# Spreading the turn of the latents and the first residual scaling in a transformer block on one Trainium2 core

## The chip, the core and the metric

The kernel runs on one core of a Trainium2 chip. A core has four engines that compute, each with its own instruction queue that is worked off in order: TensorE (matmuls and transposes, into PSUM; PE in the profile), VectorE (DVE), ScalarE (ACT) and GpSimd (POOL). SyncE (SP) issues loads from memory into the on-chip SBUF; POOL and ACT issue some as well. The engines wait for one another by semaphores. The metric is the time of one execution in microseconds (us) on the device. The unchanged kernel took 2508.15 us (median of 3 runs, 2506.3 to 2508.43).

## What is computed

One layer of a streaming encoder over 256 tokens of width 2048, in float32:

```python
h = layer_norm(ALPHA * h + 0.5 * swiglu_ffn(h, ffn1...), ln_ffn1_g, ln_ffn1_b)
mix = hybrid_mixer(h, ...)
h = layer_norm(ALPHA * h + mix, ln_mix_g, ln_mix_b)
xa = memory_cross_attention(h, mem, ...)
h = layer_norm(ALPHA * h + xa, ln_x_g, ln_x_b)
h = layer_norm(ALPHA * h + 0.5 * swiglu_ffn(h, ffn2...), ln_ffn2_g, ln_ffn2_b)
```

The mixer has two attention branches. Branch A has 16 heads of width 64 over q, k and v projected directly from h, with a relative-position bias. Branch B (latent attention) first projects h to two latents of width 512, one for q and one for k and v, and normalises each:

```python
c_q = rms_norm(q_lat, q_a_norm)     # y = x * rsqrt(mean(x^2) + eps) * gain
c_kv = rms_norm(kv_lat, kv_a_norm)
```

Its 16 heads are projected from c_q and c_kv. The outputs of both branches are gated, added and projected.

## The kernel before

Each float32 weight is split into a high part in TensorE's reduced format and the low remainder: ScalarE casts the high part (`hi`, L242, two casts of 128x1024) and VectorE subtracts it from the loaded tile to get `lo` (L245, one instruction of 128x2048). A product is then a run of `hi` matmuls and a run of `lo` matmuls. There are three load buffers (`raw`) and two each of `hi` and `lo`, so a cast has to wait until TensorE has finished the `hi` matmuls of two units earlier.

The program is a list of items, each a Python function with the weights that it needs. `add` appends one, and `run` goes through the list in order and emits the loads and splits a little ahead of the item that uses them. `add` takes `prio`: instructions emitted with SOON (400) or NEAR (100) are preferred by the framework's scheduler, which fixes each engine's order when the kernel is built, and those with LATE (-400) go behind. `held` counts weight units that an item keeps, which limits how far `run` loads ahead.

Around the change the items are, in this order:
- the projection to both latents (`w_lat`), and `lat_scale` (L849-865), which leaves the two latents, divided by their root mean square, as `self.lat`, token-major;
- `gb_apply(0, self.h)` (L434-445), with prio LATE. The residual `h` (two tiles of 128 tokens by 2048) holds the first LayerNorm's result without scale and offset, and here it gets them in place. For each quarter of 512 columns POOL loads the scale and the offset, spread over the partitions, into two work tiles (L440, L441; 256 KB each), and VectorE multiplies (L444) and adds (L445) for both token tiles. `h` is next used after the mixer's output projection;
- `kpe`: the rotary key shared by the B heads (L892-899). `swap` (L890) exchanges its halves by four small DMAs on SP's queue, and L898 waits for them;
- `a_proj(0)`, the q and k projections of the first pair of A heads (16 `hi` matmuls at L265, 16 `lo` matmuls at L267 for each), and then `lat_turn` (L868-881);
- a loop over the eight pairs of A heads: projections of the next pair, transpose of the probabilities of the pair before (L773, copied out by ScalarE at L779), scores (L921) with a softmax, output (L962, L963);
- the 16 B heads in the same manner: `b_scores` (L921, then L1037 and a softmax on VectorE and ScalarE that ends with L768), `b_trans` (L773), `b_proj` (L255, L286), `b_out` (L962, L963).

`lat_turn` transposes the latents to feature-major and applies the RMS gains: for each of the two latents and each half of its 512 features one PSUM tile is filled by two pairs of 128x128 transposes (L876). Behind each pair ScalarE multiplies by the gain into the high part (L880) and VectorE forms the low part (L881). The second pair of a tile writes the same PSUM tile as the first, and it waits until the L881 of the first pair has read it. The result `self.c` lies in the blocks X0 and X1 and is first needed by the B heads' projections. PSUM has four tiles of this kind (`at`), shared with scores, probabilities and outputs.

The work tiles `w2` (128x512) are a ring of five: the softmax tile of each head, the transposed probabilities, and both loads of a quarter in `gb_apply` come from it.

Of the kernel before, what the change touches and what calls it, by code (L numbers as in the profile page):

```python
# [17 lines left out]
P = 128  # L18
S = 256
# [27 lines left out]
SOON, NEAR, LATE = 400, 100, -400  # L47
# [44 lines left out]
class Kernel:  # L92
# [338 lines left out]
            return [scale], [quarters((0, 1))], [quarters((2, 3))]  # L431
        return steps

    def gb_apply(self, i, h):  # L434

        nc = self.nc
        for q in range(4):
            cs = slice(q * 512, (q + 1) * 512)
            g, b = self.w2(), self.w2()
            nc.gpsimd.dma_start(g, self.t["gb"][i, 0:1, cs].to_broadcast([P, 512]))  # L440
            nc.gpsimd.dma_start(b, self.t["gb"][i, 1:2, cs].to_broadcast([P, 512]))  # L441
            for tt in range(2):
                hs = h[tt][:, cs]
                nc.vector.tensor_tensor(hs, hs, g, ALU.mult)  # L444
                nc.vector.tensor_tensor(hs, hs, b, ALU.add)  # L445
# [337 lines left out]
    def mixer(self, xT, st, steps):  # L783
        nc, t = self.nc, self.t
# [24 lines left out]
        ps = {}  # L809
# [3 lines left out]
        a, b, c = steps(1)  # L813
# [51 lines left out]
                    else:  # L865
                        nc.scalar.mul(l, l, r)

        def lat_turn():  # L868
            self.c = self.act(["X0", "X1"])
            for k in range(2):  # L870
                for b in range(2):
                    ps = self.at_tile()
                    for i in range(2):
                        j, p = 2 * b + i, ps[:, i * S:(i + 1) * S]
                        for tt in range(2):
                            nc.tensor.transpose(p[:, tt * P:(tt + 1) * P],  # L876
                                                self.lat[:, tt, k, j * P:(j + 1) * P], self.ident)
                        gain = self.vec(("q_a_norm", "kv_a_norm")[k], j)
                        hi, lo = (self.c.at(half, 4 * k + j) for half in (0, 1))
                        nc.scalar.mul(hi, p, gain)  # L880
                        nc.vector.scalar_tensor_tensor(lo, p, gain, hi.bitcast(F32), ALU.mult, ALU.subtract)  # L881

        self.pair_group(0, t["w_lat"][0], 512, KT, xT, SUMS_IN, fx, lps, lqs, None, SUM_HOME + ("H5",))
        self.add(lat_scale, prio=SOON)
        self.add(lambda: self.gb_apply(0, self.h), prio=LATE)

        def swap(dst, src):

# [14 lines left out]
        qk, sc, pt = {}, {}, {}  # L903
        oA = {}

        def a_proj(i):
            def one(k):
                def fn(w):
                    ps = self.mm_tile()
                    self.mm_wide(ps, w, xT())  # L910
                    qk[i, k] = self.total(ps)
                return fn
            for k in range(2):
                self.add(one(k), t["w_qk"][i, k])

        def scores(parts, spans_q):

            ps = self.at_tile()
            for c0, tt, nk in spans_q:
                for j, (q, k) in enumerate(parts):  # L920
                    nc.tensor.matmul(ps[:, c0:c0 + nk], q[:, tt * P:(tt + 1) * P], k[:, :nk],  # L921
                                     start=(j == 0), stop=(j == len(parts) - 1))
            return ps
# [15 lines left out]
        def a_scores(i):  # L939
            def fn():  # L940
                load_rel(i + 1)
                for j in range(2):
                    bias = rel["t"][:, i % 2, j, :]
                    rows = slice(64 * j, 64 * j + 64)
                    ps = scores([(qk[i, 0][rows], qk[i, 1][rows])], CAUSAL)
                    s = self.w2()
                    with self.prio(NEAR):
                        nc.vector.scalar_tensor_tensor(s[:, :3 * P], ps[:, :3 * P], 1.0 / math.sqrt(A_DIM), bias,
                                                       ALU.mult, ALU.add)
                        self.softmax(s, SPANS)  # L950
                    sc[i, j] = s
            self.add(fn)

        def a_trans(i):
            def fn():
                for j in range(2):
                    pt[i, j] = self.transpose_p(sc.pop((i, j)), (0, P, 2 * P))
            self.add(fn)

        def pv(ps, v, pT):  # L960

            nc.tensor.matmul(ps[:, :S], v(0), pT[:, :S], start=True, stop=False)  # L962
            nc.tensor.matmul(ps[:, P:S], v(1), pT[:, S:S + P], start=False, stop=True)  # L963

        def a_out(i):
            def fn():
                if i == 0:
                    oA["t"] = self.act(["H5", "X2"])
                ps = self.at_tile()
                for j in range(2):  # L970
                    c = (2 * i + j) * A_DIM
                    pv(ps[64 * j:64 * j + 64], lambda kt: va["t"][:, kt, c:c + A_DIM], pt.pop((i, j)))
                self.split(ps[:, :S], oA["t"].at(0, i), oA["t"].at(1, i))
            self.add(fn)
# [3 lines left out]
        for g in range(2):  # L978
            def fn(w, g=g):
                if g == 0:  # L980
                    self.rt = self.block("T0")
                for j in range(4):
                    ps = self.mm_tile()
                    self.mm_feat(ps[:, :S], w, [j * 512 + k * P for k in range(4)], self.c, range(4))
                    (nc.scalar.copy if j % 2 else nc.vector.tensor_copy)(self.rt[:, 4 * g + j, :], ps[:, :S])
# [11 lines left out]

        self.add(lambda: load_rel(0))
        a_proj(0)
        self.add(lat_turn)  # L1000
        NA = A_HEADS // 2
        bq, bsc, bpt, bv, oB, kept = {}, {}, {}, {}, {}, {}

        def b_proj(h):
            def vfn(w, g=h // 4):
                if g == 0:
                    bv["t"] = self.block("X3", (P, 2, 2, 512))
                for tt in range(2):
                    ps = self.mm_tile()
                    self.mm_tok(ps, tt, w, self.c, range(4, 8), True, True)  # L1010
                    (nc.scalar.copy if tt else nc.vector.tensor_copy)(bv["t"][:, g % 2, tt, :], ps)
            if h % 4 == 0:
                self.add(vfn, t["w_v"][h // 4])

            def fn(w=None):

                if h % 2 == 0:
                    kept[h + 1] = w
                else:
                    w = kept.pop(h)  # L1020
                for k in range(2):
                    ps = self.mm_tile()
                    c = h % 2 * 1024 + k * 512
                    self.mm_feat(ps[:, :S], w, [c + j * P for j in range(4)], self.c, range(4 * k, 4 * k + 4))
                    v = self.w1()
                    (nc.scalar.copy if k == 0 else nc.vector.tensor_copy)(v, ps[:, :S])
                    bq[h, k] = v
            self.add(fn, *(() if h % 2 else (t["w_nope"][h // 2],)), held=h % 2)
# [14 lines left out]
        def b_trans(h, held):  # L1043
            def fn():
                bpt[h] = self.transpose_p(bsc.pop(h), (0, P, 2 * P))
            self.add(fn, held=held)

        def b_out(h, held):
            def fn():
                if h == 0:  # L1050
                    oB["t"] = self.act(["T1", "T2", "T3", "H4"])
                ps = self.at_tile()
                pv(ps, lambda kt: bv["t"][:, h // 4 % 2, kt, h % 4 * P:h % 4 * P + P], bpt.pop(h))
                self.split(ps[:, :S], oB["t"].at(0, h), oB["t"].at(1, h))
            self.add(fn, held=held)


        for i in range(NA + 1):
            if i + 1 < NA:
                a_proj(i + 1)  # L1060
            if i > 0:
                a_trans(i - 1)
            if i < NA:
                a_scores(i)
            if i == NA - 2:
                self.items += rope_items
            if i == NA - 1:
                b_proj(0)
                b_proj(1)
            if i > 0:  # L1070
                a_out(i - 1)
        for h in range(B_HEADS + 1):

            held = int(h % 2 and h + 2 < B_HEADS)
            if h < B_HEADS:
                b_scores(h, held)
            if h > 0:
                b_trans(h - 1, held)
            if h + 2 < B_HEADS:
                b_proj(h + 2)  # L1080
            if h > 0:
                b_out(h - 1, int(h % 2 == 0 and h + 2 < B_HEADS))


        mix, fb = Act([]), {}
# [50 lines left out]
        side = self.mem_norm()  # L1136
# [322 lines left out]
```

## Time and profile before

The profile is of one execution. It lists the busy time of each engine, then waits, a timeline per engine and the share of the chain that ended last.

| what | value |
|---|---|
| runs | 2506.3, 2508.43, 2508.15 us |
| profiled execution, span from first to last instruction | 2508.1 us |
| TensorE busy | 2484.0 us (99%) |
| VectorE busy | 2055.5 us (82%) |
| ScalarE busy | 1334.4 us (53%) |
| mean granted TensorE clock | 0.997 |

In the timeline a row is: start, length, engine, line, operation, output<-input, partitions x elements, count, and in brackets how long the engine was idle before and what released it. Consecutive instructions of one kind are merged into a row, and records of neighbouring rows overlap a little, as instructions are pipelined. In the windows view a row is a stretch, its length, and for TensorE, its weight loads, VectorE, ScalarE and GpSimd the busy time with the number of instructions; then the granted TensorE clock (1.00 is full speed), the busy share of the DMA queues, and GB/s. A wait row says who waited for whom: us in total, number of times, the longest. A DMA row ends with KB of each transfer and us from issue to landing. Line numbers are those of the kernel before; in the changed kernel lines from L869 on move by one, those behind `a_proj` by three.

### The profile page before, as it was taken

The page shows a single profiled execution, that of the slowest core. Times are in us where ns is not written, and L with a number is a line of the kernel's source. Part 1 is how long each engine was busy: PE and PEld are TensorE (multiplying, and loading weights), DVE is VectorE, ACT ScalarE, POOL GpSimd, SP SyncE. Part 2 cuts the span into 40 slices and gives each one's busy share as a digit, 9 for nine tenths or more (in the row PEclk, how much of TensorE's full clock was granted, in tenths as well). Part 3 has the DMA queues.
Part 4 walks back from the last instruction along what each step waited for, and adds up shares of the span by engine and source line. Part 5 has one row for each costly group of instructions (what it writes and reads, how often), then busy time and mean ns, then how long its engine had stood idle before and what let it go on. Part 6 is the DMA issues. An engine that isn't in the chain of part 4 may idle for free.

```text
span 2508.1 us, 30455 instructions
## 1 busy us (share of the span) xinstructions
PE 2484.0 (99%) x11966; PEld 2082.5 (83%) x11966; DVE 2055.5 (82%) x2312; ACT 1334.4 (53%) x1798; POOL 28.3 (1%) x67
## 2 busy tenths in 40 slices
PE   9999999999999999999999999999999999999998
PEld 8888888889888887888888888888888888888886
DVE  6999889899778988676578798557888988898986
ACT  5555555555455555554444564545555555555552
POOL 0000000000000001000000000000000000000000
PEclk9999999999999999999999999999999999999999
DMA  6655555546645556543456547544554555555553
GB/s 254 240 197 204 189 202 203 207 174 220 233 159 202 208 204 223 182 150 113 154 208 231 187 171 253 195 155 149 211 205 171 203 199 201 201 201 201 200 214 141
DMA packets 72512, 490.03 MB, mean 195 GB/s; under 512 B 8368, under 2 KB 8752, under 8 KB 17200
## 3 DMA queue, kind: packets, MB, share of 16 engines
q1 hardware_dynamic: 66384, 467.11, 51.7%
q0 software_dynamic: 4256, 17.83, 2.2%
q10 hardware_dynamic: 1728, 3.15, 0.3%
q8 instruction: 93, 1.52, 0.2%
q14 instruction: 51, 0.42, 0.0%
HBM read 484.77 MB, written 2.10 MB: 194 GB/s over the span
## 4 chain that ended last, share of the span: by engine, by line
PE 94%; DVE 3%; DMA 2%; ACT 0%; issue 0%; SPq 0%; DVEq 0%; POOL 0%; ACTq 0%; POOLq 0%
PE mm L299 25%; PE at L299 24%; PE mm L353 10%; PE at L353 9%; PE mm L286 8%; PE mm L265 7%; PE mm L267 4%; PE mm L255 2%; PE at L921 2%; DVE lo L245 1%; PE at L286 1%; PE at L773 1%; DMA H<-xT 0%; PE at L1275 0%; PE at L962 0%; PE at L404 0%
## 5 line engine op out<-in xcount | busy, mean ns | idle before, releaser
L242 ACT CAST hi<-raw 128x1024 fp32r<-128x1024 f32 (+1 forms) x848 | 801.9, 988 | 603.7 <-PE at L299 178.5
L245 DVE TENSOR_TENSOR lo<-raw,hi 128x2048 fp32r<-128x2048 f32 (+2 forms) x425 | 904.5, 2129 | 239.2 <-ACT hi L242 237.4
L299 PE MATMUL mm<-hi,T 128*128 128x512 f32 (+1 forms) x1280 | 298.5, 383 | 0.8 <-ACT hi L234 0.8
L242 ACT CAST X<-H 128x1024 fp32r<-128x1024 f32 (+1 forms) x162 | 165.0, 1035 | 220.2 <-DVE H L191 88.4
L299 PEld LDWEIGHTS mm<-hi,T 128*128 128x128 f32 x1280 | 238.0, 188 | 45.5 <-ACT hi L234 1.4
L299 PE MATMUL at<-hi,T 128*128 128x512 f32 x1072 | 257.3, 389 | 0.6 <-DVE w L631 0.6
L245 DVE TENSOR_TENSOR X<-H,X 128x2048 fp32r<-128x2048 f32 (+1 forms) x81 | 182.4, 2251 | 67.6 <-ACT X L242 67.6
L299 PEld LDWEIGHTS at<-hi,T 128*128 128x128 f32 x1072 | 201.1, 188 | 42.7 <-DVE w L631 1.0
L299 PE MATMUL mm<-lo,T 128*128 128x512 f32 (+1 forms) x640 | 153.8, 382 | 0.0
L299 PE MATMUL at<-hi,H 128*128 128x512 f32 x608 | 144.9, 390 | 1.0 <-DVE w L631 1.0
L299 PEld LDWEIGHTS mm<-lo,T 128*128 128x128 f32 x640 | 119.1, 188 | 21.8
L299 PEld LDWEIGHTS at<-hi,H 128*128 128x128 f32 x608 | 113.8, 188 | 25.0 <-DVE w L631 1.4
L299 PE MATMUL at<-lo,T 128*128 128x512 f32 x536 | 132.6, 389 | 0.0
L265 PE MATMUL mm<-T,hi 128*128 128x512 f32 x512 | 124.8, 394 | 0.0
L299 PEld LDWEIGHTS at<-lo,T 128*128 128x128 f32 x536 | 100.6, 188 | 20.9
L299 PE MATMUL mm<-hi,H 128*128 128x512 f32 x480 | 116.0, 391 | 0.0
L191 DVE TENSOR_TENSOR H<-H,raw 128x512 f32<-128x512 f32 (+1 forms) x162 | 109.6, 677 | 1.7
L265 PEld LDWEIGHTS mm<-T,hi 128*128 128x128 f32 x512 | 94.5, 189 | 19.3 <-issue 0.9
L299 PEld LDWEIGHTS mm<-hi,H 128*128 128x128 f32 x480 | 89.2, 188 | 18.5 <-issue 0.3
L189 DVE TENSOR_TENSOR H<-raw 128x1024 f32<-128x1024 f32 (+1 forms) x81 | 97.2, 1199 | 3.8 <-DMA raw<-ffn_w_in 3.0
L353 PE MATMUL mm<-X,X 128*128 128x512 f32 x348 | 95.8, 392 | 1.3 <-DVE H L235 1.3
L242 ACT CAST X<-raw 128x1024 fp32r<-128x1024 f32 (+1 forms) x54 | 55.3, 1036 | 52.6 <-DVE raw L191 31.4
(319 smaller groups left out, 3916.1 us busy)
## 6 DMA issues: line engine op xcount, KB each, us to landing
raw<-ffn_w_in SPq DMA_DIRECT2D x150, 1024.0 KB, 4.6
raw<-ffn_w_out SPq DMA_DIRECT2D x66, 1024.0 KB, 4.6
raw<-w_gate SPq DMA_DIRECT2D x32, 1024.0 KB, 4.7
raw<-ffn_w_out_r SPq DMA_DIRECT2D x16, 1024.0 KB, 4.8
raw<-w_qk SPq DMA_DIRECT2D x16, 1024.0 KB, 4.8
raw<-w_o_b SPq DMA_DIRECT2D x16, 1024.0 KB, 4.7
raw<-w_out SPq DMA_DIRECT2D x16, 1024.0 KB, 4.7
raw<-w_xk SPq DMA_DIRECT2D x16, 1024.0 KB, 4.8
```

Of the source, the lines that this page charges most:

```text
L189: self.nc.vector.tensor_tensor(two[0], two[1], raw[:, :m].unsqueeze(1).to_broadcast([P, 2, m]), ALU.add)
L191: self.nc.vector.tensor_tensor(t[:, a * m:a * m + m], t[:, b * m:b * m + m], raw[:, a * m:a * m + m], ALU.add)
L242: self.nc.scalar.copy(hi[:, c:d], src[:, c:d])
L245: self.nc.vector.tensor_tensor(lo[:, :n], src, hi[:, :n].bitcast(F32), ALU.subtract)
L255: self.nc.tensor.matmul(ps, w[wi][:, cols[j]:cols[j] + P], x.at(xi, kt), start=(j + wi + xi == 0), stop=(j == n - 1 and wi == 1),)
L265: self.nc.tensor.matmul(ps, hi[kt], x.both(kt), start=(kt == 0), stop=False)
L267: self.last_mm = self.nc.tensor.matmul(ps[:, :S], lo[kt], x.at(0, kt), start=False, stop=(kt == n - 1))
L286: self.last_mm = self.nc.tensor.matmul(ps, x.at(xi, kt)[:, tt * P:(tt + 1) * P], w[wi][:, j * 512:(j + 1) * 512], start=(start and j + wi ...
L299: self.last_mm = self.nc.tensor.matmul(ps[tt, g][:, :n], x.at(xi, kt)[:, tt * P:(tt + 1) * P], w[wi][:, c:c + n], start=first and j + wi + ...
L353: self.last_mm = self.nc.tensor.matmul(bank[:, :m], a[xi], v[wi][:, c * m:(c + 1) * m], start=own and first and wi + xi == 0, stop=own and ...
L773: self.nc.tensor.transpose(ps[:, i * P:(i + 1) * P], s[:, c:c + P], self.ident)
L921: nc.tensor.matmul(ps[:, c0:c0 + nk], q[:, tt * P:(tt + 1) * P], k[:, :nk], start=(j == 0), stop=(j == len(parts) - 1))
```

## The change

There are two edits. `lat_turn` is now a maker of four functions, one for each latent `k` and half `b`, and they are placed behind the four projections that follow the first pair: `a_proj(1)` takes the two of the first latent, one behind its q and one behind its k projection, and `a_proj(2)` those of the second. The ScalarE and VectorE instructions of a piece get prio NEAR. `gb_apply(0, ...)` leaves its place behind `lat_scale`; a quarter of it now stands behind each of the B heads 2, 5, 8 and 11, again with prio LATE.

```diff
-    def gb_apply(self, i, h):
+    def gb_apply(self, i, h, qs=range(4)):
...
-        for q in range(4):
+        for q in qs:
...
-        def lat_turn():
-            self.c = self.act(["X0", "X1"])
-            for k in range(2):
-                for b in range(2):
-                    ps = self.at_tile()
...
+        def lat_turn(k, b):
+            def fn():
+                if k + b == 0:
+                    self.c = self.act(["X0", "X1"])
+                ps = self.at_tile()
+                for i in range(2):
+                    j, p = 2 * b + i, ps[:, i * S:(i + 1) * S]
+                    for tt in range(2):
+                        nc.tensor.transpose(p[:, tt * P:(tt + 1) * P],
+                                            self.lat[:, tt, k, j * P:(j + 1) * P], self.ident)
+                    gain = self.vec(("q_a_norm", "kv_a_norm")[k], j)
+                    hi, lo = (self.c.at(half, 4 * k + j) for half in (0, 1))
+                    with self.prio(NEAR):
                         nc.scalar.mul(hi, p, gain)
                         nc.vector.scalar_tensor_tensor(lo, p, gain, hi.bitcast(F32), ALU.mult, ALU.subtract)
+            return fn
...
-        self.add(lambda: self.gb_apply(0, self.h), prio=LATE)
...
-        def a_proj(i):
+        def a_proj(i, side=()):
...
             for k in range(2):
                 self.add(one(k), t["w_qk"][i, k])
+                for f in side[k:k + 1]:
+                    self.add(f)
...
-        self.add(lat_turn)
...
-                a_proj(i + 1)
+                a_proj(i + 1, [lat_turn(i, b) for b in range(2)] if i < 2 else ())
...
+            if h in (2, 5, 8, 11):
+                self.add(lambda q=h // 3: self.gb_apply(0, self.h, (q,)), held=int(h % 2 == 0), prio=LATE)
```

More of the change, by code (lines that the diff above doesn't have):

```diff
@@ L866, in lat_scale @@
                         nc.scalar.mul(l, l, r)
-        def lat_turn():
-            self.c = self.act(["X0", "X1"])
-            for k in range(2):
-                for b in range(2):
-                    ps = self.at_tile()
[L873 to L879, printed above, removed]
+        def lat_turn(k, b):
[11 more added lines that the diff above has]
+                    with self.prio(NEAR):
                         nc.scalar.mul(hi, p, gain)
                         nc.vector.scalar_tensor_tensor(lo, p, gain, hi.bitcast(F32), ALU.mult, ALU.subtract)
+            return fn
         self.pair_group(0, t["w_lat"][0], 512, KT, xT, SUMS_IN, fx, lps, lqs, None, SUM_HOME + ("H5",))
         self.add(lat_scale, prio=SOON)
-        self.add(lambda: self.gb_apply(0, self.h), prio=LATE)
         def swap(dst, src):
```

## The prediction

> **What bounds the kernel now.** I read the page first, then TensorE's waits, then the timeline of each engine around the longest of them.
>
> ```profile
> span 2508.1 us, 30455 instructions
> PE 2484.0 (99%) x11966; PEld 2082.5 (83%) x11966; DVE 2055.5 (82%) x2312; ACT 1334.4 (53%) x1798; POOL 28.3 (1%) x67
> PE 94%; DVE 3%; DMA 2%; ACT 0%; issue 0%; SPq 0%; DVEq 0%; POOL 0%; ACTq 0%; POOLq 0%
> ```
>
> TensorE is busy for 99% of the span and carries 94% of the chain. The change adds and removes no matmul, so it can move the time only through moments when TensorE stands still or runs slowly. Its waits name the one that matters, and the timeline of TensorE shows it.
>
> ```profile
> PE at L876 <- DVE X L881: 5.7, 1, 5.7
> ```
>
> ```profile
> 964.74 2.08 PE L267 MATMUL mm<-T,lo 128*128 128x256 f32 x16
> 966.65 1.04 PE L876 MATMUL at<-ident,H 128*128 128x128 f32 x8
> 967.44 2.99 PE L265 MATMUL mm<-T,hi 128*128 128x512 f32 x12
> 976.11 0.69 PE L876 MATMUL at<-ident,H 128*128 128x128 f32 x2 [5.68 <-DVE X L881]
> ...
> 979.32 2.07 PE L267 MATMUL mm<-T,lo 128*128 128x256 f32 x16
> 981.22 3.82 PE L265 MATMUL mm<-T,hi 128*128 128x512 f32 x16
> 984.88 2.07 PE L267 MATMUL mm<-T,lo 128*128 128x256 f32 x16
> 986.88 0.93 PE L921 MATMUL at<-w,w 64*128 64x128 f32 x8
> ...
> 1000.61 0.66 PE L962 MATMUL at<-w,H 128*64 128x256 f32 x4
> ```
>
> This is the turn of the latents. The first halves of its four pieces (eight transposes) run at 966.65; the second halves write the same PSUM banks and must wait until VectorE's L881 has read the first. TensorE fills in 12 matmuls of the next projection, then idles 5.68 us. The windows view shows a second loss behind the idle time; in its rows PEclk is the number before the DMA share.
>
> ```profile
> 970.00:975.00 5.00, 0.43 (x2) 0.01 (x1) 5.00 (x8) 0.70 (x2) 0.54 (x1) 1.00 0.63 229
> 975.00:977.00 2.00, 0.89 (x3) 0.73 (x4) 2.00 (x5) 0.16 (x1) 0.00 (x0) 0.64 0.65 137
> 977.00:979.00 2.00, 2.00 (x10) 1.61 (x8) 1.20 (x3) 1.24 (x3) 0.00 (x0) 0.50 0.71 287
> ```
>
> The granted clock falls to 0.64 and 0.50 around and after the end of the wait. So the whole loss is read from start to start: from 966.65 to 979.32 pass 12.67 us, for 16 transposes and 16 matmuls. Eight transposes took 0.79 (966.65 to 967.44), 16 such matmuls undisturbed 3.66 (981.22 to 984.88): 2 x 0.79 + 3.66 = 5.24. **Lost: 7.4 us**, 0.30% of the span, and this is all that the turn can give back.
>
> VectorE's and ScalarE's timelines and the DMA view tell why L881 was late.
>
> ```profile
> 957.21 0.69 DVE L444 TENSOR_TENSOR h<-h,w 128x512 f32<-128x512 f32 x1 [2.23 <-DMA w<-gb]
> 968.03 0.42 DVE L898 TENSOR_TENSOR w<-w,rope 128x256 f32<-128x256 f32 x1 [3.54 <-DMA w<-w]
> 971.84 1.29 DVE L444 TENSOR_TENSOR h<-h,w 128x512 f32<-128x512 f32 x2
> 973.38 2.29 DVE L245 TENSOR_TENSOR lo<-raw,hi 128x2048 fp32r<-128x2048 f32 x1
> 975.58 2.25 DVE L881 SCALAR_TENSOR_TENSOR X<-at,vecs,X 128x256 fp32r<-128x256 f32 x5
> 999.36 2.29 DVE L245 TENSOR_TENSOR lo<-raw,hi 128x2048 fp32r<-128x2048 f32 x1 [2.08 <-ACT hi L242]
> ```
>
> ```profile
> 969.13 1.57 ACT L880 ACTIVATE X<-at,vecs 128x256 fp32r<-128x256 f32 x4
> 985.12 2.00 ACT L242 CAST hi<-raw 128x1024 fp32r<-128x1024 f32 x2 [3.21 <-issue]
> 997.33 1.99 ACT L242 CAST hi<-raw 128x1024 fp32r<-128x1024 f32 x2 [2.38 <-issue]
> 999.52 0.86 ACT L779 COPY w<-at 128x384 f32<-128x384 f32 x2
> ```
>
> ```profile
> raw<-w_qk SPq DMA_DIRECT2D x1, 1024.0 KB, 12.7
> ```
>
> ```profile
> raw<-w_qk SPq DMA_DIRECT2D x16, 1024.0 KB, 4.8
> ```
>
> VectorE waits in order for the scale loads (2.23) and for the exchange of the rotary key's halves (3.54, L898), and then has a queue before L881: two L245 splits and the gb products. ScalarE had the first pieces copied by 970.7. One weight load of that stretch took 12.7 us against a median of 4.8, and the eight gb loads were on the queues beside it.
>
> **The change, part by part.** *gb away from here.* Sixteen products (1.29 for two, so about 0.6 each, 9.6 us of VectorE) and eight POOL loads leave 952 to 990. The 2.23 wait goes with them. In the changed kernel as built, the relative-bias loads go ahead of gb on POOL's queue, and one more w_qk load stands ahead of the exchange's four small DMAs on SP's. That moves the exchange by one load at most, 4.8. VectorE does not need it early: behind L898 stands the split of a projection that TensorE reaches at about 976.
>
> *The turn in four pieces.* All 16 transposes, 8 scalings and 8 L881 remain, and the pieces stand behind four later projections. TensorE gets filler between the halves, but each piece keeps its wait, and in the built order the waiting L881 of piece 1 and piece 2 stands right behind an L245 split. So I compare, for each second half, when TensorE gets there and when L881 can be done.
> - Piece 1. Counted from the start of the lo matmuls (L267) of the projection before it: TensorE needs 1.91 for those (964.74 to 966.65), 0.2 for two transposes and 12/16 x 3.66 = 2.74 for the filler, so 4.86. The other way: the hi matmuls end 0.16 after that start (3.82 against 3.66) and free a buffer, the cast begins 0.08 later (985.04 to 985.12), the split 2.03 after it (997.33 to 999.36), L881 2.20 later (973.38 to 975.58), the transposes 0.53 after that (975.58 to 976.11): 5.00. Wait 0.15.
> - Piece 2, from the restart of piece 1. TensorE: 0.2, four matmuls 0.92, lo 1.91, transposes 0.2, the first head's scores 0.9, seven matmuls 1.60: 5.7. The other: 0.2 + 0.92 + 0.16 + 0.08 + 2.03 + 2.20 + 0.53 = 6.1. Wait 0.4.
> - Piece 3 stands ten matmuls and a softmax later: about 1.4 us of room, wait 0.
> - Piece 4: its ScalarE scaling (1.57 for four, 0.4 each) goes ahead of the two L779 copies that free the banks of the next scores. Those had 0.2 to spare (999.52 + 0.86 = 1000.38, L962 at 1000.61), so 0.2 is lost, and its own half waits 0.1.
>
> Sum of new waits: 0.9. Bounds: 0, where the filler covers all, and 3, if the exchange lands late as well (it then holds piece 1 by some 0.8) and each wait is half a microsecond longer. I take 0.9 as worked out from durations.
>
> Are waits this short charged at half clock too? A wait of 1.04 earlier in the run says no:
>
> ```profile
> 691.20 1.10 PE L404 MATMUL at<-ident,h 128*128 128x128 f32 x8 [1.04 <-DVE h L396]
> ```
>
> ```profile
> 691.20:694.00 2.80, 2.80 (x20) 2.53 (x21) 1.16 (x3) 2.80 (x6) 0.00 (x0) 1.00 0.34 143
> ```
>
> The Trainium skill (TensorE: Matmul & The Clock Gate, Part 1) says that the clock halves after an idle window of about 3.4 us and returns after a busy one; one such window at half rate is an estimated 1.7 us, where the rows give 7.4 - 5.7 = 1.7 with the pipeline's drain in it. The same page tells of a kernel whose frequent micro-idles made the clock swing, which would speak against four short waits in place of a long one; that is a rival below.
>
> *gb among the B heads.* The 9.6 us go into a stage with room, if the loads are there in time.
>
> ```profile
> 1100.00:1200.00 100.00, 100.00 (x615) 82.73 (x615) 62.06 (x141) 49.18 (x120) 0.00 (x0) 1.00 0.33 115
> ```
>
> ```profile
> DMA to landing us min/median/max: 3.5/4.8/11.2
> ```
>
> ```profile
> 1178.51 0.38 PE L963 MATMUL at<-w,X 128*128 128x128 f32 x2
> ...
> 1192.73 0.28 PE L773 MATMUL at<-ident,w 128*128 128x128 f32 x1
> ```
>
> ```profile
> 1183.49 0.55 DVE L768 TENSOR_SCALAR w<-w,sm_r 128x128 f32<-128x128 f32 x2
> ...
> 1191.82 0.55 DVE L768 TENSOR_SCALAR w<-w,sm_r 128x128 f32<-128x128 f32 x2
> ```
>
> VectorE is 62% busy there, TensorE full, the DMA queues 0.33. Each pair of loads needs two of the five work tiles. By the order of release these are a probability tile and a transposed one that the heads before have left, so the loads go out 6 to 14 us ahead of the product that reads them, against a landing of 4.8 (median) in the rows of gb. The tightest is the second load of the last quarter: its tile comes free with the head output at 1178.5 + 0.4 = 1178.9, and VectorE gets to its product after L768 (1184.0), one L444 and a copy, at 1184.9: 6.0 of room. Behind that product wait a split and the softmax of head 12, whose transpose stands at 1192.73 with the result ready at 1192.3; the built order moves that transpose 0.8 later, about what the products there add. So I take 0 for this part. Cover gone (a late load): what exceeds 6.0 goes straight to TensorE.
>
> **Sum.** 2508.1 - 7.4 + 0.9 + 0 = **2501.6**, or -0.26%. The profiled span (2508.1) and the median of the runs (2508.15) are the same for this purpose. About 0.2%, 5 us, is what a measurement of this kernel can tell from no change, so "faster" needs under 2503.1: 1.5 us to spare.
>
> **The rivals.**
> - *The waits of the pieces are larger.* For it: in two pieces L881 stands behind a split, and both paths differ by tenths only. Against: the long waits that made L881 late before (gb, the 12.7 load) are gone. With new waits of 2.4 to 5: 2503.1 to 2506, no measurable change.
> - *The stall only moves:* one piece waits through a VectorE queue as now, half of 7.4 stays: 2505. For it: L898 still blocks VectorE in order. Against: nothing that TensorE needs soon stands behind it.
> - *The clock swings* with the four short waits, the micro-idle case of the page named above. If each costs what the long one did, 1.7: 2501.6 + 4 x 1.7 = 2508.4, no change. Against it stands the row at 691.20 with its clock of 1.00.
> - *Slower: late gb loads block VectorE in the B heads.* VectorE takes its queue in order, so a late load holds splits and softmaxes and then the transposes of probabilities. For it: gb loads have taken up to 11.2. At 11.2 the last quarter loses 11.2 - 6.0 = 5.2 and the third, which has 2 to 3 more room, about 2: 2501.6 + 7 = 2509, still no change. It decides from a landing of about 14 us in these two quarters: 8 + 5 = 13 lost, over 2513. Against: the 11.2 fell where the queues were full; here they are a third busy, and the least was 3.5.
>
> **How the numbers follow.** Forecast 0.60 (2500.6 to 2503.1); larger waits or a mildly late load 0.22; the stall moves 0.06; the clock swings 0.04; slower 0.08, which also holds what I can't see. Faster is the forecast's 0.60, same 0.22 + 0.06 + 0.04 = 0.32, slower 0.08. The range begins a little under the full 7.4 (2500.7), since the runs shown reach 1.8 below their median, and ends in the second case, at 2505.5, so that less than 2 in 10 is left out.
>
> **What would show it.** Right: no wait of L876 above 0.6, a clock of 1.00 all through 950 to 1010, weight loads near 4.8 there, L444 without a wait for gb, TensorE full from 1090 to 1200. Wrong: a new wait at the second transposes of a piece above 1 us; a clock under 1 behind it; or L444/L445 waiting for gb among the heads and L773 waiting for L768 behind them.

## The result, and the profile after

The changed kernel takes 2501.01 us (median of 9 runs, 2500.04 to 2502.14), the kernel before 2507.66 us in the runs beside it (9 runs, 2506.3 to 2508.56): a ratio of 0.9973, with a 95% interval of 0.9965 to 0.9982. That is 6.65 us less, where 6.5 were forecast.

The head of the page, the busy times and the shares of the chain, of the changed kernel:

```profile
span 2500.4 us, 30460 instructions
PE 2481.8 (99%) x11966; PEld 2081.1 (83%) x11966; DVE 2055.6 (82%) x2312; ACT 1333.0 (53%) x1798; POOL 28.0 (1%) x67
PE 95%; DVE 2%; DMA 2%; issue 0%; ACT 0%; DVEq 0%; ACTq 0%
```

No engine has less to do; the span is 7.7 us shorter. TensorE's timeline where the turn stood (L876 are its transposes, L924 the scores, L965 the first head output of pair 0):

```profile
964.37 2.08 PE L267 MATMUL mm<-T,lo 128*128 128x256 f32 x16
...
971.99 2.98 PE L265 MATMUL mm<-T,hi 128*128 128x512 f32 x12
974.91 0.44 PE L876 MATMUL at<-ident,H 128*128 128x128 f32 x2
...
979.20 1.91 PE L265 MATMUL mm<-T,hi 128*128 128x512 f32 x7
981.13 0.44 PE L876 MATMUL at<-ident,H 128*128 128x128 f32 x2
...
992.43 1.34 PE L924 MATMUL at<-w,w 64*128 64x128 f32 x8
993.70 0.66 PE L965 MATMUL at<-w,H 128*64 128x256 f32 x4
...
994.51 0.51 PE L265 MATMUL mm<-T,hi 128*128 128x512 f32 x1
994.85 0.38 PE L876 MATMUL at<-ident,H 128*128 128x128 f32 x2
994.99 3.66 PE L265 MATMUL mm<-T,hi 128*128 128x512 f32 x15
```

No row has a bracket: no wait is long enough to be named. One measure serves for this and all runs below, **the stage**: from the start of the lo matmuls of the first pair's k projection (L267 at 964.37) to the start of that pair's first head output (L965 at 993.70). Before it was 964.74 to 1000.61, 35.87 us; now it is 29.33, 6.54 us less. The last two of the sixteen transposes now stand behind its end; with the wait ahead of them they take 0.25 us (994.51 to 994.99, less 0.23 for a matmul). Like for like the stage thus gives 6.3 us, nearly the whole result. The same 0.25 is missing in the stage of every run below that turns the latents in pieces with the order within a tile unchanged.

The windows view of the changed kernel, at the turn and in the B heads (columns as before; the clock is the number before the DMA share), and the DMA issues from 940 to 975, first of the kernel before, then of the changed one (KB, median us from issue to landing):

```profile
966.00:980.00 14.00, 14.00 (x85) 11.77 (x84) 7.73 (x7) 6.65 (x11) 0.00 (x0) 1.00 0.57 209
1094.00:1194.00 100.00, 100.00 (x614) 82.73 (x614) 70.69 (x158) 48.80 (x119) 4.32 (x8) 1.00 0.40 134
```

```profile
raw<-w_qk SPq DMA_DIRECT2D x5, 1024.0 KB, 6.7
w<-gb POOLq DMA_DIRECT2D x8, 256.0 KB, 7.1
...
w<-w SPq DMA_DIRECT2D x4, 32.0 KB, 7.6
```

```profile
raw<-w_qk SPq DMA_DIRECT2D x7, 1024.0 KB, 5.0
...
w<-w SPq DMA_DIRECT2D x4, 32.0 KB, 4.4
```

TensorE is full at a clock of 1.00 where it idled. Without the eight gb loads the weights land in 5.0 in place of 6.7, and the exchange of the rotary key's halves (w<-w) in 4.4 in place of 7.6. VectorE takes the products among the B heads (71% busy in these 100 us, where the prediction shows 62% for a like stretch of before), and TensorE stays full.

Both edits were made at once, so the result does not say which of them won the time. The theory on record was: L881 was late behind VectorE's queue (gb products, a late exchange, late weights), and TensorE had too little filler between the halves of a PSUM tile. The rivals are that either cause alone explains it, and inside VectorE's delay, that it was the products or the loads.

### The profile page after: what moved, and what is told of

The parts are those of the page before. It is cut to its first block, busy times and chain, and to the rows that moved or that the text cites. A ratio compares the mean times of both kernels' runs of the same rounds, so it can differ in the third digit from the quotient of the medians.

```text
span 2500.4 us, 30460 instructions
## 1 busy us (share of the span) xinstructions
PE 2481.8 (99%) x11966; PEld 2081.1 (83%) x11966; DVE 2055.6 (82%) x2312; ACT 1333.0 (53%) x1798; POOL 28.0 (1%) x67
## 4 chain that ended last, share of the span: by engine, by line
PE 95%; DVE 2%; DMA 2%; issue 0%; ACT 0%; DVEq 0%; ACTq 0%
PE mm L299 25%; PE at L299 24%; PE mm L353 10%; PE at L353 10%; PE mm L286 8%; PE mm L265 7%; PE mm L267 4%; PE mm L255 2%; PE at L924 2%; PE at L286 1%; DVE lo L245 1%; PE at L773 1%; DMA H<-xT 0%; PE at L1279 0%; PE at L965 0%; PE at L404 0%
```

## The experiments

Line numbers below shift by a few with each edit. In the rows shown the transposes are L876 throughout, and the low-part instruction is L881, L882 or L883.

**The turn in four pieces alone.** The residual's scale and offset stay behind the latents' scaling.

```diff
         self.add(lat_scale, prio=SOON)
+        self.add(lambda: self.gb_apply(0, self.h), prio=LATE)
...
-            if h in (2, 5, 8, 11):
-                self.add(lambda q=h // 3: self.gb_apply(0, self.h, (q,)), held=int(h % 2 == 0), prio=LATE)
```

> The turn in four pieces alone; the scale and offset of the residual stay where they were before, right behind the latents' scaling. Main theory (the 7.4 us at the turn came from two things together: VectorE's L881 stood late behind the products of the scale and offset, the exchange of the key's halves and a split whose weights landed late, and TensorE had only 12 matmuls of filler): the filler is there now, VectorE's queue is still long, so some of the waits at the second transposes of pieces 1 and 2 stay, 2 to 4 us in sum; 2503 to 2505, the weight load of 12.7 us is still there. Rival A (filler alone was missing): all waits at L876 under 0.6 us, 2501 to 2502, as the whole change. Rival B (the products and their loads alone were the cause): the wait only moves, one of 4 us or more with a clock under 1 behind it, 2506 to 2508.

Measured: 2507.14 us (11 runs), ratio 0.9998 (0.9989 to 1.0007): no measurable gain. The timelines of TensorE and VectorE in this run, and a window behind its wait:

```profile
971.46 1.62 PE L265 MATMUL mm<-T,hi 128*128 128x512 f32 x6
976.27 0.44 PE L876 MATMUL at<-ident,H 128*128 128x128 f32 x2 [3.20 <-DVE X L882]
```

```profile
970.20 2.28 DVE L245 TENSOR_TENSOR lo<-raw,hi 128x2048 fp32r<-128x2048 f32 x1
972.40 1.28 DVE L445 TENSOR_TENSOR h<-h,w 128x512 f32<-128x512 f32 x2
973.60 1.28 DVE L444 TENSOR_TENSOR h<-h,w 128x512 f32<-128x512 f32 x2
974.80 0.68 DVE L445 TENSOR_TENSOR h<-h,w 128x512 f32<-128x512 f32 x1
975.41 0.41 DVE L274 TENSOR_TENSOR w<-w,mm 128x256 f32<-128x256 f32 x1
975.74 0.48 DVE L882 SCALAR_TENSOR_TENSOR X<-at,vecs,X 128x256 fp32r<-128x256 f32 x1
```

```profile
977.06:980.51 3.45, 3.45 (x10) 2.71 (x9) 3.42 (x5) 0.16 (x1) 0.00 (x0) 0.51 0.32 55
```

TensorE runs out of filler after six matmuls and waits 3.20 us for a piece that stands behind a split and five products; then 3.45 us follow at a clock of 0.51. The stage is 34.15 us (963.84 to 997.99): of 6.54 us the pieces by themselves give 1.72. The stall moved, as one rival on record had it for the whole change. Of the theories, filler alone is refuted. In this build the scheduler left only six matmuls between the halves of piece 1, against twelve in the changed kernel, but six more (1.4 us) would not have covered 3.20. The wait is of the size that the main theory foresaw; the time lies in the range of the rival that blamed the products and their loads.

**Scale and offset among the B heads alone.** The latents are turned in one piece, behind the first pair's projections, as before; of the diff shown above only the edits of `gb_apply` and its place are made.

```diff
-        self.add(lambda: self.gb_apply(0, self.h), prio=LATE)
...
+            if h in (2, 5, 8, 11):
+                self.add(lambda q=h // 3: self.gb_apply(0, self.h, (q,)), held=int(h % 2 == 0), prio=LATE)
```

> Scale and offset of the residual among the B heads alone; the latents are turned in one piece, as before. Main theory: L881 is no longer behind the products, but TensorE still has only the matmuls of one projection as filler, and L881 stands behind the exchange of the key's halves; a wait of 1 to 3 us at the second transposes is left, 2502 to 2505. Rival A (filler alone was missing): the wait stays at 4 us or more, 2506 to 2508. Rival B (the products and their loads were the whole cause): no wait over 0.6 us at L876, 2501 to 2502. If the B heads paid for the products, this run would show it as well: then its gain is smaller than what the wait at L876 gives back.

Measured: 2499.67 us (6 runs), ratio 0.9969 (0.9958 to 0.9981). TensorE's and VectorE's timelines:

```profile
966.84 2.77 PE L265 MATMUL mm<-T,hi 128*128 128x512 f32 x11
969.48 0.44 PE L876 MATMUL at<-ident,H 128*128 128x128 f32 x2
...
992.92 0.66 PE L961 MATMUL at<-w,H 128*64 128x256 f32 x4
```

```profile
966.40 2.29 DVE L245 TENSOR_TENSOR lo<-raw,hi 128x2048 fp32r<-128x2048 f32 x1 [1.67 <-ACT hi L242]
968.61 0.41 DVE L274 TENSOR_TENSOR w<-w,mm 128x256 f32<-128x256 f32 x1
968.94 3.36 DVE L881 SCALAR_TENSOR_TENSOR X<-at,vecs,X 128x256 fp32r<-128x256 f32 x8
```

L881 runs at 968.94, where it stood at 975.58 before, and the second transposes follow eleven filler matmuls without a wait. VectorE even has idle time ahead of the split (1.67). The stage is 28.79 us (964.13 to 992.92), shorter than in the changed kernel. So moving the scale and offset is enough, and the one-piece turn with its filler was not too little. The main theory's wait of 1 to 3 us did not come.

**Before, with both pairs of a PSUM tile ahead of its reads.** The other way round: VectorE's work and the loads stay, TensorE's dependence goes.

```diff
                         for tt in range(2):
                             nc.tensor.transpose(p[:, tt * P:(tt + 1) * P],
                                                 self.lat[:, tt, k, j * P:(j + 1) * P], self.ident)
+                    for i in range(2):
+                        j, p = 2 * b + i, ps[:, i * S:(i + 1) * S]
                         gain = self.vec(("q_a_norm", "kv_a_norm")[k], j)
```

> Before, with one edit: the four transposes that share a PSUM bank are all issued before the bank is read, so that no second half waits for VectorE to have read the first. VectorE's queue, loads and filler are as before. Main theory: the wait of 5.68 us was this order within a bank, so it goes, and with it the low clock; a smaller wait for a free bank may follow, since four banks are held until the late L881 has read them; 2501 to 2503. Rival (what is late is VectorE's queue, whatever TensorE's order): the next use of a bank waits for L881 instead, 4 us or more at L876, L921 or another transpose, 2505 to 2508.

Measured: 2500.75 us (8 runs), ratio 0.9974 (0.9963 to 0.9984). TensorE's and VectorE's timelines:

```profile
966.36 1.91 PE L876 MATMUL at<-ident,H 128*128 128x128 f32 x16
...
979.33 0.93 PE L923 MATMUL at<-w,w 64*128 64x128 f32 x8
```

```profile
973.31 2.83 DVE L883 SCALAR_TENSOR_TENSOR X<-at,vecs,X 128x256 fp32r<-128x256 f32 x7
...
977.26 0.47 DVE L883 SCALAR_TENSOR_TENSOR X<-at,vecs,X 128x256 fp32r<-128x256 f32 x1
```

All sixteen transposes run in one go at 966.36. The low parts are formed from 973.31 to 977.7, and nobody waits: TensorE needs the PSUM tiles again only at 979.33. VectorE was less late in this execution than in that of before (973.31 against 975.58; its wait for the exchange was 1.69 in place of 3.54), but late enough: in the old order, by the rows of before (0.53 from L881 to the restart, TensorE at the second halves 3.78 behind the first), the second halves would have waited an estimated 3.7 us. The stage is 28.61 us, 7.26 below that of before. A VectorE that is this late was therefore harmful only through the order within a tile, and two added lines in the kernel before give as much as the whole change.

**The changed kernel with the same order within a tile.** The edit is the same in each piece.

```diff
                 for i in range(2):
...
+                for i in range(2):
+                    j, p = 2 * b + i, ps[:, i * S:(i + 1) * S]
                     gain = self.vec(("q_a_norm", "kv_a_norm")[k], j)
```

> The changed kernel with the same edit as the run before it: within a piece all four transposes come before the reads. Main theory: the four new waits of the pieces, about 1.0 us in sum by the trace of the changed kernel, go, and nothing else is in the way; 0.5 to 1.0 less than the changed kernel, 2500.0 to 2500.5. Rival (those waits were cover for other work, and the time moves to the next wait): same as the changed kernel within 0.3 us, 2501.

Measured: 2500.12 us (7 runs, 2499.45 to 2501.76), ratio 0.9971 (0.996 to 0.9981). The stage is 28.95 us (964.06 to 993.01), 0.38 less than in the changed kernel, and about 0.6 like for like, as all sixteen transposes lie in it. The waits at the second transposes went. What stayed is the next scores behind the fourth piece:

```profile
991.81 1.27 PE L926 MATMUL at<-w,w 64*128 64x128 f32 x8
```

They take 1.27 where the same row takes 0.93 elsewhere, probably since ScalarE's scaling (at 991.26) still goes ahead of the copies that free their tiles (at 991.63). The gain has the expected sign; against runs that scatter by 2 us it is too small to be shown by the time.

**Loads or products?** First, the products without loads, at the old place:

```diff
-        self.add(lambda: self.gb_apply(0, self.h), prio=LATE)
+        def gb_no_load():
+            for q in range(4):
+                for tt in range(2):
+                    hs = self.h[tt][:, q * 512:(q + 1) * 512]
+                    for _ in range(2):
+                        nc.vector.tensor_tensor(hs, hs, self.h[tt][:, q * 512:(q + 1) * 512], ALU.max)
+        self.add(gb_no_load, prio=LATE)
```

> Before, with the sixteen products of scale and offset replaced by sixteen VectorE instructions of the same size that read no loaded tile, and without the eight loads; the scale and offset of the residual's first LayerNorm are left out. It tells VectorE's work at this place from the traffic of its loads. Theory 1 (the 9.6 us of VectorE ahead of L881 are the cause): the wait at L876 stays at 3 us or more, with a clock under 1 behind it; 2505 to 2508. Theory 2 (the loads are the cause: VectorE's waits for them, 2.2 us, and for the exchange of the key's halves, 3.5 us, and the weights that they hold up): without loads the products run earlier, in time in which VectorE would otherwise stand still, and the wait at L876 falls under 1 us; 2500 to 2502.

Measured: 2504.05 us (10 runs), ratio 0.9986 (0.9976 to 0.9995). The run does not answer its question. With nothing to wait for, the scheduler put the sixteen instructions at 691 to 728 us, among the second LayerNorm's work, where TensorE's timeline has two waits that the other kernels do not have:

```profile
709.74 0.50 PE L286 MATMUL mm<-hi,T 128*128 128x512 f32 x1 [1.19 <-ACT T L234]
710.70 1.88 PE L286 MATMUL mm<-hi,T 128*128 128x512 f32 x7 [0.46 <-DVE T L235]
```

The stage at the turn is then 28.73 us, as with scale and offset among the B heads. So this is a second place to put them, and a worse one: of the 7.1 us that the stage gives, about 3 are lost again. TensorE reaches the stage 2.0 us later than with scale and offset among the B heads alone (966.12 against 964.13), and the two waits are 1.65 of that; where the rest is lost is not shown.

Second, the loads without the products: scale and offset among the B heads, the turn in one piece, and the eight loads once more at their old place.

```diff
         self.add(lat_scale, prio=SOON)
+        def gb_loads_unread():
+            for q in range(4):
+                cs = slice(q * 512, (q + 1) * 512)
+                for row in range(2):
+                    nc.gpsimd.dma_start(self.w2(), t["gb"][0, row:row + 1, cs].to_broadcast([P, 512]))
+        self.add(gb_loads_unread, prio=LATE)
```

> Scale and offset among the B heads, the latents turned in one piece, and beside that the eight loads of scale and offset issued once more at their old place, into work tiles that nobody reads. The other half of the run before it: traffic without work. Theory 1 (VectorE's work is the cause): no wait over 0.6 us at L876, 2499 to 2501. Theory 2 (the traffic is the cause): the weights of these projections land in 6 us or more, the exchange of the halves lands late, and a wait of 2 us or more at L876 comes back; 2503 to 2506.

Measured: 2505.9 us (10 runs), ratio 0.999 (0.9981 to 1.0). DMA issues from 940 to 975, VectorE's and TensorE's timelines (L903 is L898 of before):

```profile
raw<-w_qk SPq DMA_DIRECT2D x6, 1024.0 KB, 7.2
...
w<-w SPq DMA_DIRECT2D x4, 32.0 KB, 9.0
```

The exchange in the run with scale and offset among the B heads alone, which lacks only these loads:

```profile
w<-w SPq DMA_DIRECT2D x4, 32.0 KB, 4.3
```

```profile
969.40 0.43 DVE L903 TENSOR_TENSOR w<-w,rope 128x256 f32<-128x256 f32 x1 [5.44 <-DMA w<-w]
```

```profile
973.27 0.69 PE L876 MATMUL at<-ident,H 128*128 128x128 f32 x2 [3.64 <-DVE X L881]
```

The loads alone bring back a wait of 3.64 us, with no gb product near, as the theory of the traffic had it. The way it goes is in the rows: the four small DMAs of the exchange (32 KB), issued from 958.05 as without the loads (958.03), land after 9.0 us in place of 4.3, VectorE stands still in order for 5.44 us, and with it the split and L881 behind.

Third, the products at their old place with loads of one column each, so that they still have something to wait for:

```diff
-            cs = slice(q * 512, (q + 1) * 512)
-            g, b = self.w2(), self.w2()
-            nc.gpsimd.dma_start(g, self.t["gb"][i, 0:1, cs].to_broadcast([P, 512]))
+            cs, n = slice(q * 512, (q + 1) * 512), 512 if i else 1
+            g, b = (self.w2()[:, 0:n] for _ in range(2))
+            nc.gpsimd.dma_start(g, self.t["gb"][i, 0:1, cs][:, 0:n].to_broadcast([P, n]))
...
-                nc.vector.tensor_tensor(hs, hs, g, ALU.mult)
+                nc.vector.tensor_tensor(hs, hs, g if i else g.to_broadcast([P, 512]), ALU.mult)
```

> Before, with the sixteen products at their place and the eight loads reduced to one column each (512 bytes in place of 256 KB), which the products read again and again; the scale and offset of the first LayerNorm of the residual are wrong therefore (one value for each 512 columns). It mends the run without loads, in which the products had nothing to wait for and moved to the second LayerNorm, 250 us ahead. TensorE's order is that of before; about seven products stand between the latents' scaling and L881. Theory 1 (VectorE's work is the cause): 7 x 0.6 = 4.2 us more ahead of L881 than without them, a wait of 2 us or more at L876, 2503 to 2507. Theory 2 (the traffic is the cause, as the loads without products say): the products fill time in which VectorE waits for the casts anyway (2.1 and 1.7 us ahead of two splits without them), the weights land in 5 us, and no wait over 1 us is left at L876; 2500 to 2502.

Measured: 2504.32 us (11 runs), ratio 0.9982 (0.9973 to 0.9991). VectorE's and TensorE's timelines, and two stretches of the windows view, of the wait and of what came 1.1 us behind it:

```profile
957.31 0.69 DVE L445 TENSOR_TENSOR h<-h,w 128x512 f32<-128x512 f32 x1 [1.65 <-DMA w<-gb]
```

```profile
966.53 0.94 PE L876 MATMUL at<-ident,H 128*128 128x128 f32 x4 [0.27 <-DVE H L864]
...
972.06 0.44 PE L876 MATMUL at<-ident,H 128*128 128x128 f32 x2 [1.84 <-DVE X L881]
```

```profile
970.20:972.06 1.86, 0.02 (x2) 0.01 (x1) 1.86 (x4) 0.00 (x0) 0.00 (x0) 1.00 0.00 0
...
973.20:976.55 3.35, 3.35 (x16) 3.07 (x15) 2.94 (x6) 2.91 (x5) 0.00 (x0) 0.50 0.61 259
```

The wait lies between the two theories, the time in the range of the first. The loads alone leave a wait of 3.64 us, the products with one-column loads waits of 1.84 and 0.27. That these make 5.75 in sum, near the 5.68 of the kernel before, may be chance: each is from one execution, and the builds differ (with one-column loads the exchange stands behind one more weight load and is issued at 960.76, 2.7 us later). Nor is the third run work alone, as VectorE stands idle for 1.65 us until a one-column load has landed. What the products cost with nothing to wait for stays open. The times do not add up like the waits: the stages of these two runs are 33.02 (products) and 34.03 us (loads), which is 4.2 and 5.2 above the 28.8 without either, as each pays a stretch at half clock.

**Do the quarters matter, and how much room have the B heads?** All four quarters behind head 2, and, in another run, the changed kernel with two more VectorE instructions of the same size behind each pair of products.

```diff
-            if h in (2, 5, 8, 11):
-                self.add(lambda q=h // 3: self.gb_apply(0, self.h, (q,)), held=int(h % 2 == 0), prio=LATE)
+            if h == 2:
+                self.add(lambda: self.gb_apply(0, self.h), held=1, prio=LATE)
```

> The changed kernel, with all four quarters of the scale and offset at B head 2 in place of one quarter each at heads 2, 5, 8 and 11. It asks whether the quarters matter. Theory of the prediction (a late load holds VectorE, and what exceeds the room goes straight to TensorE; eight loads through five work tiles must wait for one another): VectorE waits for gb several times, and 9.6 us of products come within one head; 1 to 5 us more than the changed kernel, 2502 to 2506. Rival (VectorE, 62 percent busy, takes them in its idle time wherever they stand): no new wait of TensorE over 0.6 us, 2500 to 2502.

```diff
                 nc.vector.tensor_tensor(hs, hs, b, ALU.add)
+                if len(qs) == 1:
+                    for _ in range(2):
+                        nc.vector.tensor_tensor(hs, hs, hs, ALU.max)
```

> The changed kernel with twice the VectorE work in each quarter among the B heads: behind every pair of products stand two more instructions of the same size that leave the value as it is, 16 x 0.6 = 9.6 us in sum. It asks how much room is left there. Prediction's step (the B heads cover it): 0 to 1 us more than the changed kernel, 2501 to 2502. Rival (VectorE's order is tight there and what is added falls on TensorE): 3 to 10 us more, 2504 to 2511, with L773 or L965 waiting for VectorE.

Measured: 2501.01 us (8 runs, ratio 0.9976, 0.9965 to 0.9986) and 2501.72 us (10 runs, ratio 0.9976, 0.9966 to 0.9985). In the first VectorE waits once for gb, for 0.4 us, as the groups of L444 say; in the second it is 79% busy in the B heads, and TensorE full at a clock of 1.00:

```profile
DMA w<-gb: 0.4, 1
```

```profile
1094.00:1194.00 100.00, 100.00 (x615) 82.60 (x616) 78.81 (x173) 48.47 (x119) 4.33 (x8) 1.00 0.40 135
```

Neither has a new wait of TensorE. The quarters are not needed, and another 9.6 us of VectorE would fit. The expectation of 1 to 5 us for all quarters at once was wrong.

**Is there a better version?** Scale and offset among the B heads, the turn in one piece, and both pairs of a tile ahead of its reads; the edits are the second and third above.

> Both edits that sufficed by themselves: scale and offset among the B heads, the latents turned in one piece, and in it all four transposes of a bank ahead of its reads. If the turn is clean already with the first edit, nothing is left to win: 2499.5 to 2500.5, and from the first lo matmuls of the projection before the turn to the head output of pair 0 28.5 to 28.8 us, against 29.3 in the changed kernel. If the order within a bank still costs something there: 0.5 us or more less than with the first edit alone.

Measured: 2499.66 us (5 runs, 2499.34 to 2500.48), ratio 0.9964 (0.9951 to 0.9976); its stage is 28.62 us. That is 0.2 below the gb edit alone in the stage and the same in the time. Last, the changed kernel and the gb edit alone on one chip:

> The changed kernel once more, on one chip with the run that follows. If the turn in four pieces costs what the two traces say (29.3 us from the first lo matmuls to the head output of pair 0, against 28.8 in one piece), its median is 0.5 to 1.5 us above that of the next run; if the difference of 1.3 us seen between two chips was the chips', the medians agree within 0.3 us.

> Scale and offset among the B heads alone, the latents turned in one piece, beside the changed kernel on one chip. By the two traces 0.5 to 1.5 us less than the changed kernel, about 2499.7 us.

Measured: 2501.0 us (8 runs, 2499.57 to 2504.08) and 2498.97 us (6 runs, 2498.13 to 2501.37). The two timelines have stages of 29.34 (963.75 to 993.09) and 28.73 us (963.65 to 992.38). The pieces cost about 0.6 us in the stage, then, and 0.8 to 0.9 like for like. The medians are 2.0 us apart, but the runs overlap. From the stage's end to the last matmul these two traces differ by 2.6 us, and all traces of this case by 3.5 (1491.6 to 1495.1), so what the stage does not show of it stays open.

## Why the prediction was right, and where it was not

*The loss at the turn, 7.4 us: right.* Where both the wait and the low clock are gone and no piece waits (the order within a tile changed), the stage is 7.26 us shorter. That the whole came out within 0.15 us is luck: the interval of the ratio allows 4.5 to 8.8 us, and the wait was read from one execution.

*The waits of the pieces, 0.9 us: right in sum.* From start to start, piece 1 waits 974.91 - 971.99 - 2.74 = 0.18 (forecast 0.15) and piece 2 981.13 - 979.20 - 1.60 = 0.33 (0.4). Behind piece 4 the scores take 1.34 in place of 0.93, 0.41 (0.2), and its own half waits 994.85 - 994.51 - 0.23 = 0.11 (0.1). Together 1.0. About 0.1 of each difference between transposes is no wait: with scale and offset among the B heads alone the second transposes, which do not wait, follow eleven matmuls (2.51) after 2.64 (969.48 - 966.84). The comparison of whole stages, 0.8 to 0.9 like for like, agrees. None of these waits left a stretch with the clock under 1, so the rival of the swinging clock did not come about.

*gb among the B heads, 0: right, with more room than it was given.* No L444 or L445 waits for a load. Its step "what exceeds 6.0 goes straight to TensorE" was not tried by a load that was late by microseconds. Where eight loads went through five work tiles, a late one held VectorE for 0.4 us, and TensorE had no wait named; the rival of late loads was priced too high at least there.

*What the two edits do: not told apart.* The prediction gave back the 7.4 us to both edits together, with the filler between the halves as one part of it. By the runs the gb edit gives 7.08 us of the stage by itself. Like for like, the pieces give 1.5 with gb at its old place and cost 0.8 to 0.9 with gb away. What did not hold is that the pieces are needed to fill the time between the halves: the filler of one projection is enough when L881 is on time (968.94 against 975.58). The number came out right since the cost of the pieces was in the sum.

*Why L881 was late: the parts were named, not weighed.* The loads without the products bring back 5.2 of 7.1 us of the stage, the products behind one-column loads 4.2. Of the exchange's four small DMAs the prediction says that "VectorE does not need it early". In the changed kernel that is true; with the gb loads beside it, as in the kernel before, L898 is where VectorE stands longest (3.54).

*"The stall only moves"* had 0.06. For the whole change that was fair, and it is what the turn in pieces does by itself.

## What to carry to other kernels

When TensorE waits for a reader of PSUM, look first whether it must: writing a whole PSUM tile before its first read took the wait away by the order of a loop, while VectorE's reads still came late. When an engine is late, weigh the traffic of its neighbours as well as its work: loads that nobody needs for hundreds of microseconds delayed small transfers on another queue, and an engine that works in order passes such a delay on. And of two edits made at once, try each alone: here one gave everything, and the other cost a little.

## What the runs showed of the hardware

A wait of TensorE can cost more than its length, and the addition does not depend on the length. Behind waits of 5.68, 3.64, 3.20 and 1.84 us the clock stood at half for 3.41 us each time, an estimated 1.7 us lost when TensorE is busy all through it. Shorter waits left the clock at 1.00: 1.04 us at L404 in the prediction, and 1.19 and 0.46 one behind the other in the run of the products without loads. The low stretch can begin after the work has begun again: 0.8 us after the wait of 3.20 (976.27 to 977.06), 1.1 us after that of 1.84.

One reading fits all fourteen traces of this case. Within each of them the changes of the clock lie whole multiples of 3.41 us apart, as if it were decided once in every such stretch, and the clock falls at the end of a stretch in which TensorE was idle for 1.84 us or more: all of it in the kernel before and with the loads alone, 2.62 with the pieces alone, 1.84 (3.42 - 1.58) with one-column loads. The kernel before also has a stretch with 1.74 idle (3.42 - 1.68) that no fall follows. The stretches of before, the last at half clock, and then the one with one-column loads ahead of its fall at 973.20:

```profile
968.75:972.17 3.42, 1.68 (x8) 1.05 (x6) 3.42 (x5) 1.95 (x6) 0.00 (x0) 1.00 0.18 36
972.17:975.58 3.41, 0.00 (x0) 0.00 (x0) 3.41 (x4) 0.00 (x0) 0.54 (x1) 1.00 0.90 353
975.58:978.99 3.41, 2.88 (x11) 2.33 (x12) 2.62 (x7) 1.40 (x3) 0.00 (x0) 0.50 0.66 207
```

```profile
969.78:973.20 3.42, 1.58 (x11) 1.08 (x10) 3.42 (x7) 0.67 (x2) 0.00 (x0) 1.00 0.36 103
```

So by these runs what counts is the idle time within a fixed stretch, with a limit near half of it; the limit rests on one case on each side. The Trainium skill (TensorE: Matmul & The Clock Gate, Part 1) gives about 3.4 us for a busy window that brings the clock back, and these stretches agree. It also names an idle window of about 3.4 us as what lowers the clock; here 1.84 us of idle time within such a stretch sufficed.

Eight loads of 256 KB on POOL's queue slow the 32 KB transfers on SP's queue, by how much varies. The transfers landed after 4.3 and 4.4 us (medians) with scale and offset among the B heads, alone and in the changed kernel. With the eight loads beside them they took 5.0 with the pieces alone, 5.8 with both pairs ahead of the reads, 7.6 in the kernel before and 9.0 with the loads alone.
